# Projecting queries and keys of three head groups transposed, with one product moved to GpSimd and the values' matmuls ordered later

## The chip, the cores and the metric

The kernel runs on one core of a Trainium2 chip. The metric is device time in microseconds (us) of one execution. Engines are named as in the profile: PE is TensorE's matmul side and PEld its weight loads, DVE is VectorE, ACT is ScalarE, POOL is GpSimd, and SP issues nearly all DMAs. All engines take their instructions in program order, each from its own queue; the kernel is written in a tile framework that builds that order ahead of time from priorities and a timeline of its own, and inserts the semaphores.

## The reference

One residual block over 2048 rows of width 1024: RMSNorm, one projection, two kinds of attention side by side, an output projection, and a SwiGLU feed-forward part. Everything is float32. The change touches the stick-breaking half only:

```python
u = rms_norm(h, norm1_w[l])
proj = jnp.einsum('bsd,de->bse', u, w_in[l])
dq, dk, dv, sq, sk, sv = jnp.split(proj, SPLIT_POINTS, axis=-1)
...
z = jnp.einsum('bqhd,bkhd->bhqk', qb, k) * scale          # 8 heads of width 64
mask = (k_pos[None, :] < q_pos[:, None])[None, None]
log_1mb = jnp.where(mask, jax.nn.log_sigmoid(-z), 0.0)
rem = lax.cumsum(log_1mb, axis=3, reverse=True) - log_1mb
a = jnp.where(mask, jnp.exp(jax.nn.log_sigmoid(z) + rem), 0.0)
y = jnp.einsum('bhqk,bkhd->bqhd', a, v)
...
h = h + jnp.einsum('bse,ed->bsd', mix, w_out[l])
h = h + jnp.einsum('bsf,fd->bsd', jax.nn.silu(gate) * up, w_down[l])
```

In words: a weight a[t,s] is sigmoid(z[t,s]) times the product of (1 - sigmoid(z[t,j])) over the keys j between s and t. It is computed as a running product from the last key to the first.

## The kernel before

**Precision.** Matmuls run in float16 on split operands: a float32 value is a sum of a "hi" and a "lo" float16, and a product takes three of the four combinations (hi·hi, hi·lo, lo·hi). "Splitting" a tile means one cast (hi) and one subtraction (lo).

**Stages.** Eight head groups follow one another. Groups 0 to 3 are the four differential heads (`diff_attn`), groups 4 to 7 are two stick-breaking heads each (`sb_attn`). While group g is in attention, the rows of group g + 1 are projected in the gaps of PE: `advance` emits so many projection tiles (16 tiles of 128 rows each) for so much progress of the attention, and `PRI` gives the projection's matmuls a lower priority. Behind the attention of group 7 runs the output projection (`out_proj`), then the feed-forward part.

**Projection of a group** (`proj`, L379). For each tile of 128 rows `proj_tile` (L314) runs 24 matmuls: a 128x128 block of the rows, `xt`, is the stationary operand, and 384 columns of the weights stream (q, k and v of the group, 128 each). `proj_out` (L334) splits v into its tile and q, k into the tile `st`, straight out of PSUM. After every four tiles `proj_batch` (L348) turns q and k so that the head's dimensions lie on partitions: two DMA transposes (L372) write `qT[:, 2:4]` and `kT`, and two more DMAs (L374) copy `qT`'s two halves of partitions, exchanged, into `qT[:, 0:2]`. The hi parts of a head then lie on 64 partitions and the lo parts on the other 64, so that two matmuls make all four combinations. The PSUM pool `psj` has two banks, one for each tile's projection.

**Attention of a group** (`sb_attn`, L536). A unit is a block of 128 queries, i, one head, m, and a stretch, b, of up to 1024 keys: 48 units for a group. `stage_a` (L540) takes the stretch in chunks of 512 keys, the last chunk first. For each chunk `score_chunk` (L446) makes the scores with two matmuls into a PSUM bank `sc` (four banks); ACT makes 1 - beta into `om` (L554) and beta, in place in PSUM (L555); DVE makes the running product by a scan over `om` (L557) and then the product beta times the running product into `be` (L558). `split_t` (L398) splits the unit's `be`: ACT casts the hi part into the tile `s16` (three buffers), POOL subtracts for the lo part, and one DMA transpose (L403, on SP's queue) turns both into `aT` (six buffers), up to 16 blocks of 128x128. `stage_b` (L565) multiplies `aT` with v by `pv` (L453, matmuls of 64 columns at L458); it is emitted five units after its `stage_a` (`PD` = 5), and the framework is free to place it earlier or later among the scores. The tiles `be` and `om` come from one pool of nine, `z4`.

The pool `pp` has two buffers each of `st` (which groups 0 to 7 use in the projection) and `raw` (which groups 0 to 3 use there, and one step of the output weights at the end).

Of the kernel before, what the change touches and what calls it, by code (L numbers as in the profile page):

```python
# [59 lines left out]
def block(tc, a, out):  # L60
# [3 lines left out]
    with top:  # L64
# [44 lines left out]
        def nm(s):  # L109
            uid[0] += 1  # L110
            return f"{s}{uid[0]}"
# [14 lines left out]
        mhalf = c1(16, "mh")  # L126
        DVE.memset(mhalf[:], -0.5)

        def times(o, a_, b_, c=None):
# [121 lines left out]
        with ExitStack() as ph1:  # L251
# [62 lines left out]
            def proj_tile(G, xt):  # L314
# [7 lines left out]
                return pj  # L322

            def split_psum(hi, lo, src, n):
                sc = 2.0 ** -11
                if pick(A=0.84 * n + 60, D=1.05 * n + 70) == "A":
                    ACT.mul(hi, src, sc)
                else:
                    DVE.tensor_scalar(hi, src, sc, None, op0=ALU.mult)
                DVE.scalar_tensor_tensor(lo, src, sc, hi, op0=ALU.mult, op1=ALU.subtract)  # L330
                note("D", 1.05 * n + 70)

            @pri("po")
            def proj_out(g, G, pj, B, j):  # L334
# [9 lines left out]
                else:  # L344
                    split_psum(st[:, 0:4, j, 0, :], st[:, 0:4, j, 1, :], pj[:, :256].rearrange("p (c e) -> p c e", c=4), 256)

            @pri("pb")
            def proj_batch(g, G, B):  # L348
                st, v, raw = B
                qT = sp.tile([P, 4, 4, P], F16, tag="qT", bufs=QB, name=nm("qT"))  # L350
                kT = sp.tile([P, 2, 4, P], F16, tag="kT", bufs=KB, name=nm("kT"))
                if g < 4:
# [26 lines left out]
            def proj(g, G, fresh=None):  # L379
                for t in range(NT):  # L380
                    if fresh is not None:
                        feed(t)
                        xt = ahead.pop(0)
                    else:
                        xt = pp.tile([P, 2 * D], F16, tag="xt", bufs=3, name=nm("xt"))
                        SP.dma_start(xt[:], xs[t])
                    if t % 4 == 0:
                        st = pp.tile([P, 4, 4, 2, 64], F16, tag="st", name=nm("st"))
                        v = sp.tile([P, 4, 256], F16, tag="v", bufs=KB, name=nm("v"))
# [8 lines left out]
            def split_t(src, n, he="ADP", le="DP"):  # L398
# [4 lines left out]
                SP.dma_start_transpose(aT[:, : 2 * n // P, :], s16[:, : 2 * n])  # L403
                return aT
# [40 lines left out]
            @pri("sc")  # L445
            def score_chunk(G, sc, i, q, m, w, cut=False):  # L446
                for o in range(2):
                    PE.matmul(sc[:, : 128 * w].rearrange("p (t n) -> p t n", n=P), lhsT=G["q"][i // 4][:, 2 - 2 * o + m, i % 4, :], rhs=G["k"][q][:, m, 0:w, :], start=o == 0, stop=o == 1)  # L448
                if cut:
                    PE.matmul(sc[:, 128 * w - P : 128 * w], lhsT=idb[:], rhs=tri[:], start=False, stop=True, skip_group_check=True)  # L450

# [84 lines left out]
            def sb_attn(g, G):  # L536
                last = {}

                @pri("at")
                def stage_a(i, m, b):  # L540
# [8 lines left out]
                    for c in range((n - 1) // 512, -1, -1):  # L549
                        lo, hi = 512 * c, min(512 * c + 512, n)  # L550
                        w = hi - lo
                        sc = ps.tile([P, 512], F32, tag="sc", bufs=4, name=nm("sc"))
                        score_chunk(G, sc, i, 2 * b + c, m, w // P, b == i // 8 and hi == n)
                        ACT.activation(om[:, lo:hi], sc[:, :w], AF.Sigmoid, scale=G["nkz"][:])  # L554
                        ACT.activation(sc[:, :w], sc[:, :w], AF.Sigmoid, scale=G["kz"][:])  # L555
                        ov = om[:, lo:hi][:, ::-1]
                        DVE.tensor_tensor_scan(ov, ov, sc[:, :w], om[:, hi : hi + 1], op0=ALU.mult, op1=ALU.bypass)  # L557
                        DVE.tensor_tensor(be[:, lo:hi], sc[:, :w], om[:, lo + 1 : hi + 1], ALU.mult)  # L558
                        note("A", 1.7 * w + 400)
                        note("D", 3.15 * w + 350)  # L560
                    return n, split_t(be[:, :n], n, "A", "P")

                ypd = {}

                def stage_b(i, m, b, n, aT):  # L565
                    r, k = fq(g, i)
                    if i // k not in ypd:
# [660 lines left out]
```

## Time and profile before

| | |
|---|---|
| runs | 2734.09, 2731.22, 2727.44 us; median 2731.22 |
| profiled execution | 2740.3 us, its span 2738.5 us |
| mean granted TensorE clock | 0.967 |
| busy, share of the span | PE 91%, PEld 51%, DVE 72%, ACT 49%, POOL 52% |
| attention of groups 4, 5, 6, 7 begins at | 606, 794, 965, 1127 us |
| projections of groups 4, 5, 6, 7 begin at | 536, 686, 832, 987 us |
| last matmul of the values, first of the feed-forward part | 1396, 1458 us |

The attention's beginnings are those of each group's first scan (L557; there are 80 in a group), the projections' those of each group's first matmul at L320 (384 in a group). A line of the groups or of a window names first the program's line (L557), the engine and the operation, then the tiles, written and read, and the shapes; "x168" is the count; behind the bar stand the time in which any of them ran, the mean duration of one in ns, and the idle time of the engine right before them with what ended it. Matmuls are pipelined: a row's duration is longer than the distance to the next one, which is what a matmul costs in a run of them.

### The profile page before, as it was taken

To read this page: it belongs to the slowest core of one execution; us is meant where nothing else is said; L and a number is where in the kernel's file an instruction comes from. 1 tells how busy PE (TensorE), PEld (TensorE's weight loads), DVE (VectorE), ACT (ScalarE), POOL (GpSimd) and SP (SyncE) were. 2 spreads that over 40 slices of the span, in tenths; PEclk is the share of its full clock that TensorE was granted. 3 is DMA by queue.
4 is the path that set the end of the run, shared out by engine and by line. 5 is a ranking of instruction groups with operands and counts; after the bars stand their busy time and mean duration, and the time that the engine had idled before them with its cause. 6 is when DMAs were issued, how large, how long until landed. Compare 5 with 4: busy or idle time off the path is not lost.

```text
span 2738.5 us, 45414 instructions
## 1 busy us (share of the span) xinstructions
PE 2490.0 (91%) x17084; PEld 1409.8 (51%) x17084; DVE 1978.5 (72%) x3752; ACT 1353.3 (49%) x2539; POOL 1429.8 (52%) x1002
## 2 busy tenths in 40 slices
PE   7998989898978886889989898999999999999999
PEld 4655656565545553457775444444444444444444
DVE  6888879888888989987766777777786544434434
ACT  4665656566868778765644534344342212121121
POOL 2577677765554545546655566565664332222322
PEclk9999999998999997899999999999999999999999
DMA  6788787789998997997896665566657845635532
GB/s 227 199 164 178 151 198 164 180 171 200 208 201 184 212 186 151 203 192 208 213 289 256 220 234 191 208 221 216 231 204 283 316 158 181 220 128 193 192 116 93
DMA packets 646830, 543.52 MB, mean 198 GB/s; under 512 B 506369, under 2 KB 573953, under 8 KB 636369
## 3 DMA queue, kind: packets, MB, share of 16 engines
q1 hardware_dynamic: 644784, 538.53, 71.8%
q8 instruction: 134, 2.20, 0.3%
q0 software_dynamic: 512, 1.36, 0.2%
q10 hardware_dynamic: 1312, 0.72, 0.1%
q14 instruction: 88, 0.71, 0.1%
HBM read 261.08 MB, written 147.32 MB: 149 GB/s over the span
## 4 chain that ended last, share of the span: by engine, by line
PE 36%; DVE 9%; DMA 4%; POOL 3%; issue 3%; ACT 2%; SPq 0%; DVEq 0%; POOLq 0%; ACTq 0%
PE pd L1034 14%; PE pm L934 7%; PE pd L934 5%; PE pa L934 5%; DVE wd L215 2%; PE po L761 2%; DMA stages<-in_w_down_dram 1%; POOL stages L98 1%; DVE wu L215 1%; DMA aT<-s 1%; DVE z L557 1%; DVE cg L999 1%; DVE cg L98 1%; POOL s L98 1%; PE pj L320 1%
## 5 line engine op out<-in xcount | busy, mean ns | idle before, releaser
L98 POOL TENSOR_TENSOR s<-z,s 128x1024 f16<-128x1024 f32 (+7 forms) x288 | 474.4, 1655 | 320.1 <-ACT s L89 281.4
L320 PE MATMUL pj<-w,xt 128*128 128x384 f16 x3072 | 577.0, 336 | 19.2 <-DMA xt<-xs 5.6
L320 PEld LDWEIGHTS <-xt 128*128 128x128 f16 x3072 | 301.5, 101 | 233.1 <-issue 36.1
L557 DVE TENSOR_TENSOR_SCAN z<-z,sc 128x512 f32<-128x512 f32 (+3 forms) x320 | 356.1, 1114 | 72.1 <-ACT sc L555 68.8
L448 PE MATMUL sc<-kT,qT 128*128 128x512 f16 (+3 forms) x1280 | 348.3, 364 | 59.4 <-DVE z L558 23.7
L1034 PE MATMUL pd<-wd,act 128*128 128x512 f16 x1764 | 394.0, 381 | 7.2 <-DVE cu L968 7.1
L458 PE MATMUL yp<-v,aT 128*128 128x64 f16 (+1 forms) x4896 | 281.5, 209 | 82.3 <-DMA aT<-s 81.7
L458 PEld LDWEIGHTS <-aT 128*128 128x128 f16 x4896 | 245.4, 102 | 172.1 <-DMA aT<-s 110.4
L934 PEld LDWEIGHTS <-wg 128*128 128x128 f16 x1848 | 181.8, 98 | 228.1 <-issue 14.6
L934 PEld LDWEIGHTS <-wu 128*128 128x128 f16 x1848 | 180.8, 98 | 216.5 <-issue 2.0
L98 POOL TENSOR_TENSOR act<-cg,act 128x512 f16<-128x512 f32 x109 | 149.8, 1385 | 262.3 <-ACT act L993 262.3
L1034 PEld LDWEIGHTS <-act 128*128 128x128 f16 x1764 | 173.0, 98 | 216.6 <-issue 10.2
L89 ACT CAST s<-z 128x128 f16<-128x128 f32 (+7 forms) x216 | 170.3, 790 | 154.8 <-DMA aT<-s 72.9
L98 POOL TENSOR_TENSOR stages<-stages 128x512 f32<-128x512 f32 x97 | 172.9, 1783 | 120.1 <-DVE wg L215 41.4
L98 POOL TENSOR_TENSOR hs<-hs,cu 128x512 f32<-128x512 f32 x102 | 132.6, 1306 | 165.6 <-DVE hs L1040 62.7
L554 ACT ACTIVATE z<-sc,c 128x512 f32<-128x512 f32 (+3 forms) x320 | 204.4, 639 | 23.7 <-PE sc L448 18.9
L558 DVE TENSOR_TENSOR z<-sc,z 128x512 f32<-128x512 f32 (+3 forms) x320 | 193.7, 606 | 8.5
L555 ACT ACTIVATE sc<-sc,c 128x512 f32<-128x512 f32 (+3 forms) x320 | 196.5, 614 | 0.0
L1040 DVE SCALAR_TENSOR_TENSOR hs<-pd,c,hs 128x512 f32<-128x512 f32 x144 | 106.5, 748 | 118.5 <-PE pd L1034 113.6
L761 PE MATMUL po<-wo,mt 128*128 128x256 f16 x1536 | 180.7, 275 | 12.3 <-DVE xf L764 6.8
L993 ACT CAST act<-cg 128x512 f16<-128x512 f32 x126 | 76.9, 616 | 231.4 <-DVE cg L999 192.7
L934 PE MATMUL pm<-X,wu 128*128 128x512 f16 x792 | 179.1, 379 | 1.8 <-ACT cg L979 1.7
(241 smaller groups left out, 4109.1 us busy)
## 6 DMA issues: line engine op xcount, KB each, us to landing
xt<-xs SPq DMA_DIRECT2D x112, 512.0 KB, 4.4
hs<-hd SPq DMA_DIRECT2D x72, 512.0 KB, 4.5
hd<-hs SPq DMA_DIRECT2D x56, 512.0 KB, 5.8
split<-wg SPq DMA_DIRECT2D x11, 1792.0 KB, 6.9
split<-wu SPq DMA_DIRECT2D x11, 1792.0 KB, 6.7
split<-wd SPq DMA_DIRECT2D x11, 1792.0 KB, 6.8
wg<-split SPq DMA_DIRECT2D x11, 1792.0 KB, 7.4
wd<-split SPq DMA_DIRECT2D x11, 1792.0 KB, 9.1
```

Of the source, the lines that this page charges most:

```text
L89: ACT.copy(dst, src)
L98: (DVE if e == "D" else POOL).tensor_tensor(dst, a_, b_, op)
L320: PE.matmul(pj[:, :384], lhsT=xv[:, xi, kt, :], rhs=G["w"][:, wi, kt, :], start=n == 0, stop=n == 23)
L448: PE.matmul(sc[:, : 128 * w].rearrange("p (t n) -> p t n", n=P), lhsT=G["q"][i // 4][:, 2 - 2 * o + m, i % 4, :], rhs=G["k"][q][:, m, 0:w, ...
L458: PE.matmul(yp[:, y0 : y0 + wd], lhsT=aT[:, a_, :], rhs=v[:, v_ : v_ + wd], start=start and j == 0 and q == 0, stop=stop and j == nb - 1 a ...
L554: ACT.activation(om[:, lo:hi], sc[:, :w], AF.Sigmoid, scale=G["nkz"][:])
L555: ACT.activation(sc[:, :w], sc[:, :w], AF.Sigmoid, scale=G["kz"][:])
L557: DVE.tensor_tensor_scan(ov, ov, sc[:, :w], om[:, hi : hi + 1], op0=ALU.mult, op1=ALU.bypass)
L558: DVE.tensor_tensor(be[:, lo:hi], sc[:, :w], om[:, lo + 1 : hi + 1], ALU.mult)
L761: PE.matmul(po[:, sl], lhsT=mt[:, kt, P * xi : P * xi + P], rhs=wos[2 * h + n][wi][:, kt, :], start=q == 0, stop=q == 23)
L934: PE.matmul(ps_[:].rearrange("p (t n) -> p t n", n=P), lhsT=wv[:, wo, wi, 128 * kt : 128 * kt + 128], rhs=X[xo][:, :, xi, kt, :], start=st ...
L1034: PE.matmul(po[:], lhsT=act[:, ao, xi, 128 * j : 128 * j + 128], rhs=W["d"][:, wo, wi, :], start=start and u == 0 and q == 0, stop=u == nu ...
```

## The change

It has four parts, for groups 4 to 6 unless said otherwise.

1. `proj_turned` and `turned_out` take the place of `proj_tile`, `proj_out` and `proj_batch`. For q and k the weights are stationary and 128 rows stream, so q and k come out already turned; v is made as before. That is 72 matmuls of 128 columns for a tile instead of 24 of 384. q and k of two tiles share one PSUM bank, v of two tiles the other; both are emptied after the second tile. The splits write `qT` and `kT` directly; q is multiplied by a column, `half`, that is zero on the other head's partitions. The DMAs of `proj_batch` go, and `score_chunk` makes three matmuls for a chunk in place of two.
2. In chunks with c = 1 (the second 512 keys of a stretch) beta is written to `be` in SBUF, not in place in PSUM, and the product (L558) runs on POOL in place of DVE.
3. In groups 4 and 5 two of five units take `s16` from the tag `raw` and one of four takes `aT` from the tag `st`: five buffers in place of three, and eight in place of six.
4. In all four groups `stage_b`'s matmuls are put, on PE's queue, behind the last score matmul emitted so far. `stage_b` is emitted seven units after its `stage_a` in groups 4 and 5 (`lag` = `PD` + 2), five after in groups 6 and 7.

```diff
+        half = c1(2, "half")
+        DVE.memset(half[:], 0.0)
+        for m in range(2):
+            DVE.memset(half[64 * m : 64 * m + 64, m : m + 1], 2.0 ** -11)
...
+            def turned(g):
+                return 4 <= g < NG - 1
+
+            @pri("pm")
+            def proj_turned(G, xt, pq, pv, r):
+                xv = xt[:].rearrange("p (s k n) -> p s k n", s=2, k=KT)
+                for c in range(3):
+                    n = 0
+                    for kt in range(KT):
+                        for xi, wi in ((0, 0), (0, 1), (1, 0)):
+                            w_, x_ = G["w"][:, wi, kt, 128 * c : 128 * c + 128], xv[:, xi, kt, :]
+                            o = pv[:, P * r : P * r + P] if c == 2 else pq[:, 256 * c + P * r : 256 * c + P * r + P]
+                            PE.matmul(o, lhsT=x_ if c == 2 else w_, rhs=w_ if c == 2 else x_, start=n == 0, stop=n == 23)
+                            n += 1
+
+            @pri("po")
+            def turned_out(pq, pv, qT, kT, v, j):
+                two = slice(j - 1, j + 1)
+                q2, k2 = (pq[:, 256 * c : 256 * c + 256].rearrange("p (t n) -> p t n", t=2) for c in range(2))
+                for m in range(2):
+                    ACT.mul(qT[:, m, two, :], q2, half[:, m : m + 1])
+                    DVE.scalar_tensor_tensor(qT[:, 2 + m, two, :], q2, half[:, m : m + 1], qT[:, m, two, :], op0=ALU.mult, op1=ALU.subtract)
...
+                split_psum(kT[:, 0, two, :], kT[:, 1, two, :], k2, 256)
+                vv = v[:, two, :].rearrange("p t (h s e) -> p t h s e", h=2, s=2)
+                split_psum(vv[:, :, :, 0, :], vv[:, :, :, 1, :], pv[:, :256].rearrange("p (t h e) -> p t h e", t=2, h=2), 256)
...
+                        if t % 2 == 0:
+                            pq, pv_ = (psj.tile([P, 512], F32, tag="pj", name=nm("pj")) for _ in range(2))
+                        proj_turned(G, xt, pq, pv_, t % 2)
+                        if t % 2 == 1:
+                            turned_out(pq, pv_, qT, kT, v, t % 4)
...
-                s16 = s16p.tile([P, 2048], F16, tag="s16", bufs=SB, name=nm("s16"))
+                if wide is not None and wide % 5 in (1, 3):
+                    s16 = pp.tile([P, 4, 256], F32, tag="raw", name=nm("s16"))[:].rearrange("p t n -> p (t n)").bitcast(F16)
...
-                aT = sp.tile([P, 16, P], F16, tag="aT", bufs=AB, name=nm("aT"))
+                if wide is not None and wide % 4 == 3:
+                    aT = pp.tile([P, 4, 4, 2, 64], F16, tag="st", name=nm("aT"))[:].rearrange("p c t s e -> p (c t) (s e)")
...
-                for o in range(2):
-                    PE.matmul(sc[:, : 128 * w].rearrange("p (t n) -> p t n", n=P), lhsT=G["q"][i // 4][:, 2 - 2 * o + m, i % 4, :], rhs=G["k"][q][:, m, 0:w, :], start=o == 0, stop=o == 1)
+                terms = ((m, 0), (2 + m, 0), (m, 1)) if turned else ((2 + m, m), (m, m))
+                for o, (a_, b_) in enumerate(terms):
+                    last = PE.matmul(sc[:, : 128 * w].rearrange("p (t n) -> p t n", n=P), lhsT=G["q"][i // 4][:, a_, i % 4, :], rhs=G["k"][q][:, b_, 0:w, :], start=o == 0, stop=o == len(terms) - 1)
...
+                lag = PD + 2 if g < NG - 2 else PD
...
+                        front.append(score_chunk(G, sc, i, 2 * b + c, m, w // P, b == i // 8 and hi == n, turned(g)))
+                        aside = c == 1 and turned(g)
+                        beta = be[:, lo:hi] if aside else sc[:, :w]
-                        ACT.activation(sc[:, :w], sc[:, :w], AF.Sigmoid, scale=G["kz"][:])
+                        ACT.activation(beta, sc[:, :w], AF.Sigmoid, scale=G["kz"][:])
...
-                        DVE.tensor_tensor(be[:, lo:hi], sc[:, :w], om[:, lo + 1 : hi + 1], ALU.mult)
+                        (POOL if aside else DVE).tensor_tensor(be[:, lo:hi], beta, om[:, lo + 1 : hi + 1], ALU.mult)
...
+                    return n, split_t(be[:, :n], n, "A", "P", wide[0] if g < NG - 2 else None)
...
                 def stage_b(i, m, b, n, aT):
+                    with tc.issue_after(front[-1]):
+                        stage_c(i, m, b, n, aT)
...
-                            if len(pend) > PD:
+                            if len(pend) > lag:
```

`stage_c` is the body that `stage_b` had. The numbers by which the framework's balance of work between engines is reckoned (`note`) change with the work.

More of the change, by code (lines that the diff above doesn't have):

```diff
@@ L345, in proj_out, with new_qk @@
                     split_psum(st[:, 0:4, j, 0, :], st[:, 0:4, j, 1, :], pj[:, :256].rearrange("p (c e) -> p c e", c=4), 256)
+            def new_qk():
+                qT = sp.tile([P, 4, 4, P], F16, tag="qT", bufs=QB, name=nm("qT"))
+                kT = sp.tile([P, 2, 4, P], F16, tag="kT", bufs=KB, name=nm("kT"))
+                return qT, kT
             @pri("pb")
@@ L349, in proj_batch @@
                 st, v, raw = B
[L350 to L351 removed]
+                qT, kT = new_qk()
                 if g < 4:
@@ L445, in score_chunk @@
             @pri("sc")
-            def score_chunk(G, sc, i, q, m, w, cut=False):
-                for o in range(2):
-                    PE.matmul(sc[:, : 128 * w].rearrange("p (t n) -> p t n", n=P), lhsT=G["q"][i // 4][:, 2 - 2 * o + m, i % 4, :], rhs=G["k"][q][:, m, 0:w, :], start=o == 0, stop=o == 1)
+            def score_chunk(G, sc, i, q, m, w, cut=False, turned=False):
+                terms = ((m, 0), (2 + m, 0), (m, 1)) if turned else ((2 + m, m), (m, m))
+                for o, (a_, b_) in enumerate(terms):
+                    last = PE.matmul(sc[:, : 128 * w].rearrange("p (t n) -> p t n", n=P), lhsT=G["q"][i // 4][:, a_, i % 4, :], rhs=G["k"][q][:, b_, 0:w, :], start=o == 0, stop=o == len(terms) - 1)
                 if cut:
-                    PE.matmul(sc[:, 128 * w - P : 128 * w], lhsT=idb[:], rhs=tri[:], start=False, stop=True, skip_group_check=True)
+                    last = PE.matmul(sc[:, 128 * w - P : 128 * w], lhsT=idb[:], rhs=tri[:], start=False, stop=True, skip_group_check=True)
+                return last.ins
             @pri("pv")
```

28 lines of the change are left out of this document (23 added, 5 removed).

## The prediction

> **What bounds the kernel now.** I read the page first: PE is busy for 91% of the span. That is no answer for the stages that change, so I cut the run into windows at the first scan of each group. Each row gives the stretch, its length, the busy time (and count) of PE, PEld, DVE, ACT and POOL, the granted clock, the DMA engines' share and GB/s.
>
> ```profile
> 536.00:606.00 70.00, 66.50 (x541) 43.03 (x542) 65.89 (x196) 43.67 (x114) 46.92 (x33) 0.98 0.78 159
> 606.00:794.00 188.00, 161.97 (x1598) 102.53 (x1596) 166.12 (x309) 146.22 (x287) 102.03 (x63) 0.94 1.02 207
> 794.00:965.00 171.00, 140.20 (x1420) 86.83 (x1418) 151.78 (x268) 133.61 (x252) 86.20 (x54) 0.91 0.99 195
> 965.00:1127.00 162.00, 123.71 (x1299) 76.04 (x1296) 149.52 (x251) 131.17 (x246) 83.86 (x55) 0.85 0.87 173
> ```
>
> These are the end of group 3's attention and the attentions of groups 4, 5 and 6. In groups 4 and 5 the DMA engines are at 1.02 and 0.99 (packets overlap, so the share can pass 1); in group 6 they are at 0.87, and DVE is at 149.52 of 162 us. Then the waits of 606 to 1127 us (who, on what: total, times, longest) and that stretch's DMAs:
>
> ```profile
> POOL s L98 <- ACT s L89: 217.1, 101, 7.2
> PEld L458 <- DMA aT<-s: 61.5, 54, 3.4
> PE yp L458 <- DMA aT<-s: 44.8, 42, 2.9
> ACT s L89 <- DMA aT<-s: 44.0, 34, 3.9
> DVE z L557 <- ACT sc L555: 38.0, 42, 4.6
> PE sc L448 <- DVE z L558: 18.3, 21, 2.4
> ```
>
> ```profile
> DMA packets 266988, 100.18 MB, mean 192 GB/s; under 512 B 244321, under 2 KB 258740, under 8 KB 266932
> q1 hardware_dynamic: 266932, 99.44, 95.6%
> qT<-qT SPq DMA_DIRECT2D x24, 128.0 KB, 2.7
> aT<-s SPq DMA_TRANSPOSE x146, 4.4
> qT<-st SPq DMA_TRANSPOSE x12, 3.4
> kT<-st SPq DMA_TRANSPOSE x12, 3.7
> ```
>
> The transpose of the weights, `aT`, is late for two readers: PE, which has the values' matmuls in its queue ahead of the next scores, and ACT, whose cast wants an `s16` buffer back. While ACT stands, the sigmoids behind the cast stand, and DVE's scan waits for those (38.0 us). So groups 4 and 5 are held by the transposes' round trip, group 6 by DVE.
>
> **The change part by part.**
>
> *DMAs that go.* A batch of four tiles has two transposes of 128x1024 float16 (0.524 MB) and two copies of 128 KB (0.262 MB). By bytes, 99.44 MB cost 0.956 x 521 = 498 us, so 0.786 MB cost 3.9 us; by packets, 2048 transposed rows of 256 bytes and 128 of 2 KB at 498 / 266932 us cost 4.1 us. I take 4.0. How many batches lie in each stage follows from the projection's matmuls in it, 96 to a batch:
>
> ```profile
> 606.00:794.00 188.00, 100.05 (x521) 51.71 (x522) 0.94 1.02 207
> 794.00:965.00 171.00, 75.83 (x407) 39.87 (x404) 0.91 0.99 195
> 965.00:1127.00 162.00, 44.34 (x240) 22.81 (x240) 0.85 0.87 173
> ```
>
> That is 5.4, 4.2 and 2.5 batches, the last partly group 7's, which keep their DMAs: 22, 17 and about 4 us of DMA time go. 1.02 x 188 = 192 becomes 170, 169 becomes 152, 141 becomes 137. Their issue goes from SP's queue too, where `aT`'s transposes stand behind it.
>
> The Trainium skill's page "DMA: Bandwidth & Descriptors", section "Latency and other measured facts", gives a DMA transpose 261 GB/s; 0.524 MB would then cost 2.0 us against 2.7 at the 192 GB/s of the row above, and the relief in groups 4 and 5 would be some 7 us less in all. The row is of this kernel, mixed with its other packets, so I stay with it.
>
> *DVE and POOL.*
>
> ```profile
> L557 DVE TENSOR_TENSOR_SCAN z<-z,sc 128x512 f32<-128x512 f32 x224 | 285.3, 1274 | 37.1 <-ACT sc L555 35.3
> L558 DVE TENSOR_TENSOR z<-sc,z 128x512 f32<-128x512 f32 x224 | 153.6, 686 | 5.2
> L98 POOL TENSOR_TENSOR hs<-hs,cu 128x512 f32<-128x512 f32 x102 | 132.6, 1306 | 165.6 <-DVE hs L1040 62.7 <-DVE cu L1040 45.4 <-issue 44.8
> L98 POOL TENSOR_TENSOR s<-z,s 128x1024 f16<-128x1024 f32 x120 | 262.6, 2193 | 153.9 <-ACT s L89 146.3 <-issue 4.0 <-POOL s L98 1.2
> L330 DVE SCALAR_TENSOR_TENSOR v<-pj,v 128x128 f16<-128x128 f32 x128 | 35.2, 278 | 10.6 <-ACT v L327 10.4
> L330 DVE SCALAR_TENSOR_TENSOR st<-pj,st 128x256 f16<-128x256 f32 x64 | 26.0, 408 | 2.9 <-ACT st L327 2.9
> L327 ACT ACTIVATE st<-pj 128x256 f16<-128x256 f32 x64 | 24.9, 393 | 13.7 <-DVE v L330 13.4 <-PE sc L450 0.3
> ```
>
> Chunks with c = 1 hold, for one head, 1280 columns in blocks 4 to 7, 2048 in 8 to 11, 2048 + 1280 in 12 to 15: 6656, for two heads 13312, or 26 chunks of 512 (32 instructions). DVE loses 26 x 0.686 = 17.8 us a group. POOL gains 26 x 1.306 = 34 us: 102, 86 and 84 become 136, 120 and 118. POOL stands idle for 217 us behind the casts, so there is room; ahead of the product nothing but POOL's own subtraction can stand, behind it that unit's cast waits. Emptying two projected tiles takes DVE 4 x 408 in place of 2 x (278 + 408): +0.26 us, 2 us a group; ACT the same. Net, DVE goes from 166, 152, 150 to 150, 136, 134; ACT from 146, 134, 131 to 148, 136, 133. Writing beta to SBUF and not PSUM I bound by the two sigmoids' rows, 705 to SBUF and 681 ns to PSUM at 512 columns: under 1 us a group, taken as nothing.
>
> *PE.* The next rows are start, length and count; a matmul costs the distance to the next piece's start.
>
> ```profile
> 579.32 1.95 PE L458 MATMUL yp<-v,aT 128*128 128x128 f16 x32
> 581.10 1.14 PE L320 MATMUL pj<-w,xt 128*128 128x384 f16 x6
> ...
> 822.01 0.60 PE L448 MATMUL sc<-kT,qT 128*128 128x512 f16 x2
> 822.44 0.98 PE L458 MATMUL yp<-v,aT 128*128 128x64 f16 x28
> 823.26 1.95 PE L320 MATMUL pj<-w,xt 128*128 128x384 f16 x11
> ...
> 825.43 2.28 PE L320 MATMUL pj<-w,xt 128*128 128x384 f16 x13
> 827.54 0.25 PE L458 MATMUL yp<-v,aT 128*128 128x64 f16 x3
> ```
>
> 128 columns with a new stationary block each cost 1.78 / 32 = 56 ns, 384 cost 2.11 / 13 = 162, a score of 512 costs 215, a values' matmul 29. A projected tile goes from 24 x 162 = 3.89 us to 72 x 56 = 4.03: +2 us a group. The third score pass is 34816 columns a group, 68 x 0.215 = 14.6 us. In all 17 us a group, 50 in the three. PE's columns now (projection + 136 x 0.215 + some 820 x 0.029) are 137, 119 and 92 us; they become 154, 136 and about 108. With 188, 171 and 162 us to lie in, the addition hides behind DMA, DVE and ACT; if that cover goes, it costs up to 50.
>
> *Emptying PSUM.* Both `psj` banks serve one pair of tiles, so the next pair waits for six reads (three on ACT, three on DVE, some 0.4 us each, among scans of 1.3). Nothing shows this wait; nothing to 2 us for each of 24 pairs. PE can run scores and values meanwhile, except under group 3's attention, where PE is busy for 66.5 of 70 us: I take +2 us there. `load_w` takes its `psj` bank after tile 8, so in the middle of a pair, and now waits for that pair to be emptied; its weights are wanted eight tiles later, some 80 us, so I cost that at nothing.
>
> *More buffers, later values.*
>
> ```profile
> L403 SPq DMA_TRANSPOSE aT<-s x288: 1167/1782/6046, 113.9 to 1388.4; - x144
> DMA to landing us min/median/max: 2.3/4.3/9.0
> ```
>
> A transpose lands in 4.3 us (9.0 at most). Seven units at the stages' 188 / 48 = 3.9 and 3.6 us are 25 us from scores to values, so the 45 us of PE's waits and the 44 of ACT's should mostly go in groups 4 and 5. What is late next is ACT: a full unit has two chunks of 705 + 681 ns and a cast of 1053, about 3.8 us.
>
> ```profile
> L554 ACT ACTIVATE z<-sc,c 128x512 f32<-128x512 f32 x224 | 157.9, 705 | 16.8 <-PE sc L448 14.9 <-PE sc L450 1.4 <-POOL s L98 0.4
> L555 ACT ACTIVATE sc<-sc,c 128x512 f32<-128x512 f32 x224 | 152.5, 681 | 0.0
> L89 ACT CAST s<-z 128x1024 f16<-128x1024 f32 x83 | 87.4, 1053 | 71.3 <-DVE z L558 19.7 <-DMA aT<-s 15.2 <-issue 13.7
> ```
>
> The new order makes PE hold ready values back while scores wait for a bank of `sc`; those waits are 18.3 us now and should get shorter with the shorter DVE. `finish` moves with the values: its transposes on PE, and behind them its few DVE, ACT and POOL instructions and one DMA of 256 KB on SP for four blocks of queries come up to two units later, past the next units' transposes on SP; nobody reads `ms` before group 7, so nothing there. In group 7 the last values come up to two units later (each 24 x 0.029 = 0.7 us): +1.5.
>
> *Sum.* Group 4: next bounds are DMA 170, PE 154, DVE 150; 188 becomes 172 (-16). Group 5: DMA 152, DVE 136, PE 136; 171 becomes 157 (-14). Group 6: DMA 137, DVE 134, ACT 133; today's 12 us above its busiest engine grow to about 18, as it has no more buffers and a third score pass: 162 becomes 155 (-7). With +2 and +1.5 that is -33.5. The profiled execution took 2740.3 us, 9 above the median of the runs shown, 2731.2; so 2707 for a profiled run, 2698 for the median.
>
> **The rivals.**
>
> 1. *The third pass is bare.* For it: PE waits for DVE before scores (18.3 us) and its order is now fixed. Against it: PE's columns fill at most 154 of 172 us. Half of 50 us on the path: -33.5 + 25, 2722.
> 2. *The transposes never bound.* The page "Perfetto Trace Analysis" of the Trainium skill, section "Identifying the Most-Contended Engine", calls the DMA engines' occupancy misleading; by it my 1.02 proves nothing. As a mechanism: the latency of a transpose, not the engines' load, made the waits, and the buffers and DVE alone help. Then groups 4 and 5 give some 5 us each: -17 + 3.5, 2717. Against it: landing takes 4.3 us at the median, 2.3 at least.
> 3. *POOL's queue, the slower one.* The new product may stand behind a subtraction that waits for ACT's cast; that cast waits for a product. POOL waits 217.1 / 101 = 2.15 us a time there. If of each of the 96 new products more than 33.5 / 96 = 0.35 us stays on the path, the gain is gone; a quarter of 2.15 gives 96 x 0.54 = 52, so 2731 - 33.5 + 52 = 2750. For it: the 7.2 us at the longest. Against it: product and last chunk run apart, and nine `z4` tiles hold four units.
> 4. *Weight loads bind.* 72 loads a tile at 98 ns, one after the other, would be 7.1 us against 3.9: 150 us in 48 tiles, half of it bare: over 2770. The run of 32 above, at 56 ns with a load each, speaks against it.
> 5. *Nothing comes of it*: ACT, at 148 of 172, holds each stage where it is: 2731.
>
> **How the numbers follow.** The forecast has 0.58 (alone 2675 to 2718: all of 50 us relieved, or 13). Rival 1 has 0.15, rival 2 0.08, rival 3 0.13, rival 4 0.03, rival 5 0.03. About 0.2%, 5.5 us, can be told from no change. Faster: 0.58 + 0.10 of rival 1 + 0.07 of rival 2 = 0.75; slower: 0.13 + 0.03 + 0.02 of rival 1 + 0.02 of rival 5 = 0.20; the rest, 0.05, the same. The range reaches from a little under the forecast's own, 2668, to rival 3's 2752, and leaves out about 0.1 above and 0.03 below.
>
> **What would show it.** Right: in the attentions of groups 4 and 5 the DMA share under 0.95, PE's and ACT's waits on `aT` together under 30 us, DVE about 16 us less in each stage, L458 waiting for nothing. Wrong: POOL's product waiting on POOL's subtraction with ACT's cast behind it (rival 3); PE above 95% busy with long runs at the score line (rival 1); the projection's matmuls of 128 columns more than 60 ns apart (rival 4); pairs of tiles waiting for `psj`.

## The result and the profile after

The changed kernel takes 2706.61 us at the median (2704.82 to 2710.16, four runs); the kernel before took 2732.65 (2727.44 to 2736.76, four runs). The ratio is 0.9907 with a 95% interval of 0.9894 to 0.992: 26 us, just under 1%, faster. The forecast was 2698, 33.5 us faster than the 2731.2 that it started from. The profiled execution of the changed kernel has a span of 2702.7 us.

The page after, and the attentions of groups 4, 5 and 6 cut at their first scans (stretch, length, PE, PEld, DVE, ACT, POOL, clock, DMA share, GB/s):

```profile
span 2702.7 us, 50511 instructions
PE 2500.8 (93%) x19628; PEld 1502.5 (56%) x19628; DVE 1956.5 (72%) x3711; ACT 1346.4 (50%) x2488; POOL 1516.4 (56%) x1097
```

```profile
602.00:762.00 160.00, 145.90 (x2227) 118.37 (x2224) 148.18 (x256) 138.93 (x259) 123.26 (x92) 0.98 0.94 185
762.00:920.00 158.00, 141.26 (x2237) 113.89 (x2235) 143.99 (x250) 132.73 (x242) 116.21 (x88) 1.00 0.95 185
920.00:1092.00 172.00, 153.31 (x2096) 115.62 (x2092) 151.26 (x267) 131.37 (x238) 117.96 (x89) 0.97 0.92 187
```

Group 4 went from 188 to 160 us, group 5 from 171 to 158, group 6 from 162 to 171. The DMA engines fell from 1.02 and 0.99 to 0.94 and 0.95 although the stages are shorter; PE's clock rose from 0.94, 0.91 and 0.85 to 0.98, 1.00 and 0.97. The main waits of 602 to 1092 us (line numbers are now those of the changed kernel: L341 is the turned projection, L363 the lo parts out of its banks, L506 the scores, L517 the values, L619 the second sigmoid, L621 the scan, L622 the product):

```profile
POOL z L622 <- DVE z L621: 64.0, 49, 4.0
POOL s L98 <- ACT s L89: 49.1, 40, 4.9
ACT s L89 <- DMA aT<-s: 18.9, 12, 3.6
PEld L517 <- DMA aT<-s: 13.6, 15, 2.4
PE sc L506 <- DVE z L622: 12.1, 17, 1.6
PE yp L517 <- DMA aT<-s: 10.4, 12, 2.3
```

PE's wait on `aT` fell from 44.8 to 10.4 us, ACT's from 44.0 to 18.9. POOL's wait for ACT's cast fell from 217.1 to 49.1 us; it now waits mainly for the scan (L621) that feeds its new product (L622).

### The profile page after: what moved, and what is told of

Its sections match the earlier page's. It is cut to its first block, busy times and chain, and to the rows that moved or that the text cites. A ratio compares the mean times of both kernels' runs of the same rounds, so it can differ in the third digit from the quotient of the medians.

```text
span 2702.7 us, 50511 instructions
## 1 busy us (share of the span) xinstructions
PE 2500.8 (93%) x19628; PEld 1502.5 (56%) x19628; DVE 1956.5 (72%) x3711; ACT 1346.4 (50%) x2488; POOL 1516.4 (56%) x1097
## 5 line engine op out<-in xcount | busy, mean ns | idle before, releaser
L506 PE MATMUL sc<-kT,qT 128*128 128x512 f16 (+3 forms) x1520 | 381.6, 353 | 53.5 <-DVE z L622 19.0
L621 DVE TENSOR_TENSOR_SCAN z<-z,sc 128x512 f32<-128x512 f32 (+3 forms) x320 | 352.8, 1112 | 56.7 <-ACT sc L619 34.9
L325 PE MATMUL pj<-w,xt 128*128 128x384 f16 x1920 | 353.1, 332 | 17.2 <-ACT raw L374 5.9
L1004 PEld LDWEIGHTS <-wg 128*128 128x128 f16 x1848 | 181.5, 98 | 226.1 <-issue 12.4
L1004 PEld LDWEIGHTS <-wu 128*128 128x128 f16 x1848 | 181.5, 98 | 220.2 <-issue 7.1
L517 PE MATMUL yp<-v,aT 128*128 128x64 f16 (+1 forms) x4896 | 269.1, 204 | 37.3 <-DMA aT<-s 36.2
L517 PEld LDWEIGHTS <-aT 128*128 128x128 f16 x4896 | 236.9, 99 | 115.4 <-DMA aT<-s 47.7
L325 PEld LDWEIGHTS <-xt 128*128 128x128 f16 x1920 | 187.5, 99 | 146.9 <-issue 23.3
L98 POOL TENSOR_TENSOR stages<-stages 128x512 f32<-128x512 f32 x97 | 171.6, 1769 | 119.1 <-DVE wg L220 41.3
L618 ACT ACTIVATE z<-sc,c 128x512 f32<-128x512 f32 (+3 forms) x320 | 210.6, 663 | 25.1 <-PE sc L506 12.5
L506 PEld LDWEIGHTS <-qT 128*128 128x128 f16 x1520 | 128.2, 99 | 121.4 <-issue 23.5
L341 PE MATMUL pj<-xt,w 128*128 128x128 f16 x2304 | 176.9, 222 | 6.2 <-DVE v L363 5.2
```

What stands on the lines that cost most here:

```text
L98: (DVE if e == "D" else POOL).tensor_tensor(dst, a_, b_, op)
L325: PE.matmul(pj[:, :384], lhsT=xv[:, xi, kt, :], rhs=G["w"][:, wi, kt, :], start=n == 0, stop=n == 23)
L341: PE.matmul(o, lhsT=x_ if c == 2 else w_, rhs=w_ if c == 2 else x_, start=n == 0, stop=n == 23)
L506: last = PE.matmul(sc[:, : 128 * w].rearrange("p (t n) -> p t n", n=P), lhsT=G["q"][i // 4][:, a_, i % 4, :], rhs=G["k"][q][:, b_, 0:w, :] ...
L517: PE.matmul(yp[:, y0 : y0 + wd], lhsT=aT[:, a_, :], rhs=v[:, v_ : v_ + wd], start=start and j == 0 and q == 0, stop=stop and j == nb - 1 a ...
L1004: PE.matmul(ps_[:].rearrange("p (t n) -> p t n", n=P), lhsT=wv[:, wo, wi, 128 * kt : 128 * kt + 128], rhs=X[xo][:, :, xi, kt, :], start=st ...
```

## The experiments

All ratios are to the kernel before, on the same chip, with their 95% intervals. The table gathers the stages from one profiled execution of each kernel, from first scan to first scan, in us; group 7 ends at its last scan. "Turned" is the turned projection with its three score passes, "product" the product on POOL, "order" the values behind the scores, "buffers" the extra `s16` and `aT` with the seven units.

| kernel | ratio | group 4 | 5 | 6 | sum | group 7 |
|---|---|---|---|---|---|---|
| before | 1 | 187.5 | 171.6 | 162.0 | 521 | 255 |
| turned alone | 1.0009 | 179.5 | 168.5 | 176.7 | 525 | 250 |
| product alone | 1.0006 | 185.4 | 165.4 | 154.5 | 505 | 265 |
| product, order | 0.9925 | 186.6 | 161.5 | 151.2 | 499 | 250 |
| product, order, five `s16` | 0.9979 | 183.4 | 167.4 | 158.0 | 509 | 264 |
| turned, product, order | 0.9956 | 166.1 | 162.0 | 178.3 | 506 | 257 |
| turned, product, buffers | 0.9954 | 169.1 | 166.3 | 177.2 | 513 | 261 |
| turned, buffers | 1.0033 | 181.5 | 169.2 | 181.8 | 532 | 259 |
| turned, order, buffers | 1.0149 | 177.6 | 183.6 | 193.2 | 554 | 263 |
| all (the changed kernel) | 0.9907 | 160.2 | 158.2 | 171.4 | 490 | 258 |

One caution stands over the table. Group 7 has almost the same work in all of them, and its stage takes 250 to 265 us. The framework places the whole program anew after each edit, and I take these 15 us for what placing alone can move in a total; no run shows that by itself. I therefore read the parts from the stages they touch, and a difference of 15 us between two totals is not yet evidence for a mechanism.

**1. Without the product on POOL.**

```diff
-                        aside = c == 1 and turned(g)
+                        aside = False
```

> The changed kernel with the c = 1 products back on DVE; everything else of the change stays. Theory (DVE's relief is needed, ACT and DVE are the next bounds): DVE's busy time in the attentions of groups 4, 5, 6 goes back up by 18 us each, from 148, 144, 151 to about 166, 162, 169, and the stages, now 160, 158 and 171 us, can't be shorter than that: some 25 us of the 26 gained are lost, ratio to before 0.998 to 1.003. Rival 3 (the product on POOL costs waits): the kernel gets faster without it, ratio 0.988 or less. Rival 2 (DVE was not what counted): ratio stays at 0.990 to 0.993.

Measured: ratio 1.0149 (1.0129 to 1.0169), 41 us slower than the kernel before. The product is worth some 67 us inside the changed kernel, more than the DVE work it takes away, and the theory was 25. (The edit also puts beta of these chunks back into its PSUM bank, which stays in use until DVE's product is done; no run separates this from the work that DVE takes back.) DVE is near its limit, at 92%, in group 4 alone:

```profile
609.00:786.00 177.00, 152.81 (x2287) 123.72 (x2285) 162.07 (x277) 142.74 (x267) 98.88 (x62) 0.96 0.84 174
786.00:970.00 184.00, 144.50 (x2072) 115.00 (x2070) 155.13 (x265) 136.04 (x251) 85.40 (x54) 0.92 0.76 151
970.00:1163.00 193.00, 163.91 (x2233) 123.89 (x2234) 163.59 (x286) 141.62 (x268) 88.80 (x57) 0.96 0.79 172
```

In groups 5 and 6 DVE is at 84 and 85%, the DMA engines at 0.76 and 0.79: something else holds these stages. Experiment 12 came from this.

**2. Without the extra buffers and the seven units; 3. without the order; 4. without the turned projection (and the buffers).**

```diff
-                lag = PD + 2 if g < NG - 2 else PD
+                lag = PD                                  # 2 and 4, with split_t's wide = None
...
-                    with tc.issue_after(front[-1]):       # 3
-                        stage_c(i, m, b, n, aT)
+                    stage_c(i, m, b, n, aT)
...
-                return 4 <= g < NG - 1                    # 4, the product on POOL kept
+                return False
```

> The changed kernel without the two tags' extra buffers and with the values five units behind in all groups; the order on PE stays. Theory (the transposes' round trip is what the buffers hide, in groups 4 and 5): the waits of PE and ACT on aT, 17 us in these two groups now, come back in part, to 30 to 50 us, and 8 to 15 us are lost: ratio 0.9935 to 0.996. If the order on PE alone, with five units, is enough (group 6 has no more than that and its waits on aT are 13 us): ratio 0.990 to 0.992, no loss.

> The changed kernel without the order on PE's queue: the values are emitted seven and five units after their scores, but the framework may place their matmuls earlier. Theory (the framework believes the transposes earlier than they land and puts values ahead of scores that could run): in groups 4 and 5, where the delay falls back to some five units, PE's waits on aT rise from 5 us to 15 to 30, and 5 to 10 us are lost: ratio 0.9925 to 0.9945. Rival (the order only ties PE's hands): the same or faster, 0.9905 or less.

> The kernel before with the c = 1 products on POOL and the order on PE, values five units behind; the projection, the DMAs of q and k and the two score passes are as before, so it differs from the kernel without the extra buffers by the turned projection alone. Theory (the DMA engines bind groups 4 and 5): slower than that kernel by 12 to 25 us, DMA share back at 1.0 in group 4; ratio 0.999 to 1.003. Rival 1 (the third score pass is bare): faster than that kernel by up to 15 us, ratio 0.986 to 0.990. Rival 2 (the DMA engines' load never bound): within 5 us of it.

Measured: 0.9956 (0.9944 to 0.9969), 0.9954 (0.9938 to 0.9969) and 0.9925 (0.9912 to 0.9938). Without the buffers 13 us go, within the expected range; without the order 13 us go, more than the expected 5 to 10. Where the order is missing, PE stands before late transposes again, in the waits of 600 to 1113 us of that kernel:

```profile
PEld L517 <- DMA aT<-s: 63.2, 45, 5.5
PE yp L517 <- DMA aT<-s: 52.0, 40, 5.0
ACT s L89 <- DMA aT<-s: 23.2, 16, 3.4
```

The fourth kernel is a miss for the theory: it is faster than the second, from which it differs by the turned projection alone, by about 0.3%. It bears out none of the three expectations whole. Group 4 does get longer with the old projection, 166 to 187 us, as the DMA theory has it, with the DMA share back at 0.97. But group 5 stays at 162, at the same share, and group 6 gets shorter, 178 to 151. The first rows are the stages with the old projection; the next count the projection's matmuls in each stage of the changed kernel, whose group 7 projects at L325 as before:

```profile
604.00:791.00 187.00, 159.23 (x1577) 102.78 (x1574) 158.52 (x305) 138.42 (x255) 128.97 (x95) 0.95 0.97 206
791.00:952.00 161.00, 134.36 (x1419) 85.30 (x1419) 142.36 (x261) 128.42 (x232) 111.75 (x86) 0.96 0.97 204
952.00:1103.00 151.00, 119.90 (x1268) 73.87 (x1268) 135.28 (x235) 126.66 (x229) 111.86 (x86) 0.86 0.86 184
```

```profile
602.00:762.00 160.00, 71.00 (x1110) 64.35 (x1110) 0.98 0.94 185
762.00:920.00 158.00, 71.21 (x1124) 64.14 (x1121) 1.00 0.95 185
920.00:1092.00 172.00, 54.46 (x793) 49.28 (x793) 0.97 0.92 187
...
920.00:1092.00 172.00, 28.93 (x168) 15.92 (x168) 0.97 0.92 187
```

At 72 (turned) and 24 matmuls a tile the changed kernel projects 15, 16 and 18 tiles in the three stages; the kernel before, and the one with the old projection, project 22, 17 and 10. The old projection runs far ahead under group 4 and leaves ten tiles for group 6; the turned one spreads evenly. So the turned projection moves eight tiles, some 32 us of PE, out of groups 4 and 5 into group 6, and one stage alone misprices it.

The fourth kernel says more: the product and the order alone, with the old projection and all its DMAs in place, give 20 of the 26 us. What the turned projection and the buffers add to it together is 5 us, by ratios whose intervals overlap.

**5. The DMAs put back as load.**

```diff
+                if j == 3 and g >= 5:
+                    bh = bias[:].rearrange("p h n -> p (h n)").bitcast(F16).rearrange("p (s c n) -> p s c n", s=2, n=P)
+                    d2 = sp.tile([P, 7, P], F16, tag="d2", bufs=1, name=nm("d2"))
+                    for q in range(2):
+                        SP.dma_start_transpose(bh[:, q], v[:].rearrange("p t n -> p (t n)"))
+                    for o in (0, 64):
+                        SP.dma_start(d2[o : o + 64].rearrange("p c n -> p (c n)"), bh[64 - o : 128 - o, 0, 0:7].rearrange("p c n -> p (c n)"))
```

> The changed kernel, and for each batch of four tiles of groups 5 and 6 (8 of the 12 batches) two DMA transposes of 128x1024 float16 and two copies (112 KB each) are issued on SP as before the change, from v into space that nobody reads: their load without anybody's wait. 8 x 4.0 us = 32 us of DMA time come back between 602 and 1092 us. Theory (the DMA engines' load binds groups 4 and 5, now at 0.94 and 0.95): DMA share at 1.0 or over, some 12 to 20 us lost, ratio 0.995 to 0.998. Rival 2 (only the latency of a transpose counted, and the buffers hide it): 4 us at most, ratio 0.9905 to 0.992.

Measured: 0.9962 (0.9948 to 0.9976), 15 us lost. The total is within the theory's range; the stages do not bear the theory out. The rows are the three stages, then the put-back transposes issued in each of them (two to a batch), then what SP's queue waited for at the transposes (L360) and the copies (L362) that were put back (L628 is the scan in this kernel):

```profile
601.00:760.00 159.00, 145.15 (x2234) 117.91 (x2232) 145.90 (x252) 138.94 (x259) 123.99 (x93) 0.99 0.94 189
760.00:920.00 160.00, 141.27 (x2235) 114.24 (x2233) 143.86 (x248) 132.71 (x240) 116.34 (x88) 0.99 1.05 197
920.00:1102.00 182.00, 157.35 (x2102) 118.22 (x2099) 152.56 (x277) 133.36 (x240) 118.92 (x89) 0.96 0.92 199
```

```profile
bias<-v SPq DMA_TRANSPOSE x2, 3.9
bias<-v SPq DMA_TRANSPOSE x8, 4.3
bias<-v SPq DMA_TRANSPOSE x6, 4.3
```

```profile
SPq L360 <- DVE z L628: 7.0, 5, 3.1
SPq L362 <- DMA bias<-v: 4.1, 3, 1.9
SPq L360 <- DVE z L614: 3.4, 2, 2.3
SPq L360 <- DVE y L493: 2.2, 1, 2.2
```

By shares and lengths the DMA engines work 485 us here against 459 in the changed kernel, 26 us for eight batches of 0.75 MB: 3.3 us each, where the prediction took 4.0 for 0.79 MB. Four batches fall into group 5's stage. They bring 18 us of DMA time and a share of 1.05, and the stage grows by 2.5 us, from 158.2 to 160.7. Group 4's stage, with one batch, gets 2 us shorter. Of the 11 us lost in the three stages 10.5 lie in group 6, where the share is 0.92 as in the changed kernel. So a share above 1 did not hold group 5, and what the 15 us are stays open. Nor is it load alone that was put back: SP's queue, in which `aT`'s transposes stand behind the new DMAs, waited 17 us at them. Rival 2 and the placing both remain.

**6. Two score passes in place of three.**

```diff
-                terms = ((m, 0), (2 + m, 0), (m, 1)) if turned else ((2 + m, m), (m, m))
+                terms = ((m, 0), (2 + m, 0)) if turned else ((2 + m, m), (m, m))
```

> The changed kernel with two score passes in groups 4 to 6: the product of q's hi part with k's lo part is left out. 44 us of PE go. If the third pass hides behind DMA, DVE and ACT, as forecast: 5 us at most, ratio 0.9885 to 0.9907. Rival 1 (it is bare, for half or more): 15 to 35 us faster, ratio 0.978 to 0.985; that the kernel with the old projection was 8 us faster than its turned pair points this way.

Measured: 0.9892 (0.9872 to 0.9911), some 4 us faster than the changed kernel, whose 0.9907 lies inside this interval; the sum of the three stages is 489 against 490. The 44 us of the third pass are hidden but for about that much, and rival 1, which had 15 to 35 us, falls. The pass does move work: without it 19, 17 and 14.5 tiles are projected in the three stages (15, 16 and 18 with it), group 6 falls from 171 to 166 us and group 4 grows from 160 to 167.

**7. The product on POOL alone; 8. the turned projection alone.** Number 7 is the kernel before with the product's lines of the diff; number 8 is the changed kernel with the edits of 1, 2 and 3 together.

> The kernel before with the c = 1 products of groups 4 to 6 on POOL and nothing else. DVE loses 18 us a group. If the DMA engines bind groups 4 and 5, these barely move and group 6 gains some 10: ratio 0.995 to 0.997. If DVE's work was what counted in all three groups, as the 67 us that the product was worth in the changed kernel suggest: 20 us or more, ratio 0.990 to 0.9927, and the order on PE, which is what this lacks against the kernel with 0.9925, is worth little without the turned projection.

> The kernel before with the turned projection (and the three score passes) in groups 4 to 6 and nothing else: products on DVE, no order on PE, three and six buffers, values five units behind. Theory as formed by now: the turned projection by itself costs time, since its pair of tiles keeps both PSUM banks until DVE and ACT have emptied them, and a busy DVE empties late; then the projection is barely ahead of the attention and the attention waits for it. Slower than before by 20 to 45 us, ratio 1.007 to 1.017, with the last projected tile less than 15 us ahead of the block that needs it, where it was 40 to 120 us ahead before. The forecast's step (22 + 17 + 4 us of DMA time go, 17 us of PE a group hide): faster, ratio 0.990 to 0.996.

Measured: 1.0006 (0.9993 to 1.0018) and 1.0009 (0.9993 to 1.0024). Neither does anything to the total by itself, and none of the expected ratios came. With the turned projection alone the lead over the attention did fall, to 10 us at the least in group 6, and cost nothing in the total. The two profiles suggest why (first the product alone, then the turned projection alone):

```profile
605.00:790.00 185.00, 157.12 (x1539) 99.34 (x1538) 157.79 (x302) 137.82 (x255) 126.92 (x93) 0.96 1.00 205
790.00:955.00 165.00, 133.99 (x1458) 84.26 (x1455) 141.59 (x260) 130.30 (x230) 114.62 (x87) 0.98 1.03 206
955.00:1110.00 155.00, 122.51 (x1268) 76.93 (x1268) 136.20 (x237) 127.07 (x230) 112.66 (x86) 0.85 0.92 178
```

```profile
601.00:781.00 180.00, 154.30 (x2331) 125.39 (x2329) 165.33 (x283) 144.34 (x271) 95.66 (x62) 0.96 0.85 174
781.00:949.00 168.00, 144.31 (x2232) 116.17 (x2230) 155.33 (x264) 135.63 (x250) 87.18 (x54) 0.98 0.84 170
949.00:1126.00 177.00, 152.27 (x2039) 111.31 (x2037) 161.03 (x283) 138.75 (x264) 88.66 (x57) 0.97 0.85 182
```

With the product moved, the DMA engines stand at 1.00 and 1.03 and groups 4 and 5 take 185 and 165 us. With the DMAs gone, the share is 0.85, but DVE is at 91 to 92% of each stage and groups 4 and 5 take 180 and 168. I read this as two limits side by side, either of which alone holds the stage. The table agrees in group 4: 188 us before, 183 to 187 in the kernels with the product and the old projection, 178 to 182 in the turned ones without the product, 160 to 169 with both. In groups 5 and 6 it shows no such pattern, and group 6 is longer in every turned kernel than in the kernel before.

That the one limit is the DMA engines' load is not shown. With the turned projection six tiles, some 24 us of PE, leave group 4 as well. And the share is not a fixed load: the product alone and the product with the order move the same 99 MB in the three stages, and by shares and lengths this took 498 us in the one and 467 in the other.

The product alone did shorten the three stages by 16 us; group 7, which it does not touch, took 10 us more.

**9. Five `s16` buffers without the turned projection.** The kernel of number 4, with `raw` as in the change for groups 4 to 6.

> The kernel before with the c = 1 products on POOL, the order on PE, values five units behind, and five buffers of s16 in groups 4 to 6 (from the tag raw): the parts of the change that need no turned projection. ACT waited 44 us for an s16 there with three buffers; if a third to a half of that was on the path, 8 to 15 us are gained on 0.9925: ratio 0.987 to 0.9895, faster than the changed kernel. If the DMA engines bind (0.97 in groups 4 and 5), buffers move nothing: 0.992 to 0.9925.

Measured: 0.9979 (0.997 to 0.9989), slower than the same kernel with three buffers, 0.9925. The expected 8 to 15 us did not come; by the table 9 us were lost in the three stages and 14 in group 7. The buffers add no instruction, so I suspect the placing. What exactly went wrong I have not settled.

**10. More room in PSUM for the pairs; 11. emptying first.** The changed kernel projects barely ahead of the attention: from the last matmul of a tile's projection to the first score of that block of queries there pass 9 us at the least in group 6, where it was 96 us before. I took this for a new limit, and the two banks of the pairs for its cause. In the edits, the first pair of lines is number 10, the second number 11.

```diff
-                            pq, pv_ = (psj.tile([P, 512], F32, tag="pj", name=nm("pj")) for _ in range(2))
+                            pq, pv_ = psj.tile([P, 512], F32, tag="pj", name=nm("pj")), ps.tile([P, 512], F32, tag="pvb", bufs=1, name=nm("pvb"))   # and "sc" has bufs=3
...
-PRI = {"sc": 0, "spl": 0, "pv": 0, "fin": 0, "pm": -200, "po": 0, "pb": 0, "lw": 0, "fr": 0, "at": 200, "ox": 0, "wm": 0}
+PRI = {"sc": 0, "spl": 0, "pv": 0, "fin": 0, "pm": -200, "po": 400, "pb": 0, "lw": 0, "fr": 0, "at": 200, "ox": 0, "wm": 0}
```

> The changed kernel with q and k of the pairs alone in the two psj banks, v in a bank of its own that is taken from the scores (three sc banks in place of four, in all groups). If the banks hold the projection back, it gets ahead of the attention again (over 20 us at the least, where it is 9 us in group 6 now), and group 6's stage falls from 171 us to some 160: ratio 0.985 to 0.989, less what a bank fewer costs the scores. If PE itself, full at 150 of 160 us, holds it back: no gain, and the missing sc bank costs 5 to 15 us, ratio 0.9925 to 0.997.

> The changed kernel with the emptying of the projection's banks put ahead of other work in the framework's order (the priority po from 0 to 400; in all groups). The time from a pair's last matmul to its q and k emptied, 4.8 us at the median now and 12.5 at the most, falls; if the banks hold the projection back, group 6's stage falls by 5 to 10 us, ratio 0.987 to 0.9895. If PE holds it back: within 4 us of the changed kernel, 0.990 to 0.992.

Measured: 1.0045 (1.003 to 1.0059) and 0.9989 (0.9975 to 1.0003). With its own banks the projection does get ahead, to 71 us at the least in group 6, and its work goes back under groups 4 and 5 (the turned projection's matmuls in each stage):

```profile
611.00:784.00 173.00, 86.13 (x1335) 77.13 (x1333) 0.98 0.92 186
784.00:949.00 165.00, 81.95 (x1250) 73.02 (x1248) 0.98 0.95 180
949.00:1122.00 173.00, 22.81 (x347) 19.87 (x344) 0.95 0.82 179
```

Group 6 still takes 173 us, with only five turned tiles left in it beside eight of group 7's. Not having the projection ahead is not what holds the changed kernel; this theory falls, as far as a run can say that also took a bank from the scores. In the eleventh, emptying took no less time (5.3 us at the median, 4.8 before the edit), and 15 of its 22 us were lost before group 4's first scan, in groups that the change does not touch but whose emptying the new priority covers too.

**12. Without the product and without the order.** The edits of 1 and 3 together.

> The changed kernel with the c = 1 products back on DVE and without the order on PE's queue: turned projection, more buffers, values emitted seven and five units after their scores. It asks why the changed kernel without the POOL product lost 1.5% against the kernel before, when the turned projection alone lost nothing. If the order on PE does it (with DVE slow, PE holds ready values back while scores wait for DVE): the loss goes, ratio 0.996 to 1.003, and group 6's stage falls from 193 us to some 177. If the buffers and the seven units do it: ratio 1.010 or more.

Measured: 1.0033 (1.0016 to 1.005). Without the product on POOL, taking the order away gains 32 us, where with the product it loses 13. Its stages come to 532 against 554 us. The ratio is just above the range expected if the order does it, and group 6 is at 182 rather than 177. Waits that differ, in the kernel with the order (786 to 1163 us) and in the one without (781 to 1131 us); "issue" is idle time in which the engine waited for nothing that the profile shows:

```profile
DVE z L621 <- ACT sc L619: 37.3, 24, 6.5
PEld L341 <- issue: 25.5, 10, 6.3
PE pj L341 <- DVE v L363: 22.7, 6, 6.2
PE yp L517 <- DMA aT<-s: 4.4, 4, 2.4
```

```profile
PE yp L517 <- DMA aT<-s: 15.7, 17, 3.5
DVE z L621 <- ACT sc L619: 13.7, 16, 3.2
PEld L341 <- issue: 8.6, 10, 3.9
PE pj L341 <- DVE v L363: 1.6, 3, 0.7
```

The order saves 11 us of waits on `aT` and costs 21 us of waits of the projection for a bank that DVE has not emptied, up to 6.2 us at a time; I take it that the next scores, and so the scan, stand behind them. The weights' step of `load_w`, which takes the same banks, waits 12 us for one with the order and 5 without. Where DVE is relieved the emptying comes in time: in the changed kernel the projection waits 5 us for its banks in all three stages. This is how the rows read; that the banks' waits alone make the 32 us was not tried.

## Why the prediction was right

**The whole.** -33.5 us was forecast and -26 measured, in the forecast's own range. In the profiled pair the three stages went from 521 to 490, -31 against -37 forecast. The total was right; of the mechanism a part was borne out, a part was not, and some luck was in it, as follows. The product and the order, without the part that was to relieve the DMA engines, give 20 of the 26 us (4).

**DMAs.** 22 + 17 + 4 = 43 us of DMA time were to go. By shares and lengths the three stages had 502 us and now have 459: 43. The match is closer than such sums can bear, as the same bytes took 498 and 467 us in two kernels (7). That this load bound groups 4 and 5 is not shown: put back, it cost 15 us, but not in the stage in which most of it landed (5). Rival 2's mechanism stays open, though not its 5 us a group. The Trainium skill, "Perfetto Trace Analysis", section "Identifying the Most-Contended Engine", calls the occupancy of the DMA engines misleading; here the trace agrees: group 5 went to a share of 1.05 and grew by 2.5 us.

**DVE and POOL.** The direction was right, the size was not. The sum of DVE was to fall from 468 to 420; it fell from 467 to 443. The product itself went as reckoned: 96 of them took 91 us on POOL, 30 us a group against 34. But the step "DVE loses 17.8 us a group, and emptying costs 2" left out the program's own balance: `split_psum` picks the engine of each hi part by reckoned load, and with DVE relieved on paper it chose DVE. That line's 17 us on DVE are most of the 23 that are missing. These rows are the line on ACT before (606 to 1127 us; it had none on DVE), then on DVE and on ACT after (602 to 1092 us):

```profile
606.00:1127.00 521.00, 33.16 (x98) 0.90 0.96 192
```

```profile
602.00:1092.00 490.00, 16.97 (x43) 0.98 0.94 186
...
602.00:1092.00 490.00, 4.24 (x9) 0.98 0.94 186
```

**PE.** A matmul of 128 columns with its own weights takes 56 ns in the turned projection too:

```profile
710.70 2.96 PE L341 MATMUL pj<-xt,w 128*128 128x128 f16 x50
713.49 0.67 PE L341 MATMUL pj<-w,xt 128*128 128x128 f16 x9
```

The next piece starts 2.79 us later, and 2.79 us for 50 is 56 ns; rival 4 falls. The cover of the third pass was real (6).

**Buffers and order.** Under 30 us of waits on `aT` were forecast for PE and ACT together in groups 4 and 5, and 17 came. The two parts are worth 13 us each, in the company of the other parts. Of the other signs, the DMA share came to 0.94 and 0.95, the second not quite under 0.95; DVE lost 18 us in group 4 but 8 in group 5, where 16 was forecast; and the values' matmuls still waited 5 us for `aT` in the two groups.

**The stages, where the sum was mis-sized.** Group 4 gave -27 for -16, group 5 -13 for -14, group 6 +9 for -7. The step that failed is "PE's columns", which left the 5.4, 4.2 and 2.5 batches where they were: the projection no longer runs ahead, and eight tiles moved into group 6. The third pass is a part of it, since without it 3.5 of the eight left group 6 again (6), and the pairs' banks are another, since with a bank of its own for v five did (10). That these tiles make group 6's +9 is not shown: in number 10 the stage stayed at 173 us without the five, though with one score bank fewer. In the sum the two errors met, 11 us too much gained in group 4 and 16 too little in group 6; that is luck.

**The small terms.** In the changed kernel's three stages PE waits 5 us for the pairs' banks, where nothing to 2 us a pair was allowed, and 6 us for `load_w`'s, which was put at nothing. Group 3's end was to lose 2 us and gained 4; group 7's end lost 3 where 1.5 was said, within what placing alone moves.

**Rival 3.** POOL's product hardly held up the unit: in groups 4 and 5 ACT's cast waited 3.5 us for it and 4.1 for POOL's subtraction. Without the product the other three parts together lose 41 us (1).

## What to carry to other kernels

Where two resources of a stage stand within a few per cent of each other, an edit that relieves one can come to nothing, and that is no verdict on the edit: try the two together before dropping either, and also without the rest, since two of the four parts gave most of the gain here. When a load is put back that nobody waits for, see in which stage it lands and in which one the time is lost, and whether the queue that issues it is held up as well; the total alone does not tell throughput from latency. And price a change in the sum of the stages that share its work, since work without a due date moves to wherever the other engines leave room.

## What was not expected

The same order on PE's queue gained 13 us in one company and lost 32 in another. The product of two SBUF tiles took POOL 1135 ns for 512 columns, where the sum of two float32 tiles elsewhere in this kernel takes 1306; what makes the difference is not shown. And an ACT cast out of PSUM with a column as its scale took 519 ns for 256 columns, against 396 with a constant in the kernel before; that the column makes the difference was not tried.

```profile
L622 POOL TENSOR_TENSOR z<-z,z 128x512 f32<-128x512 f32 x60 | 68.1, 1135 | 46.3 <-DVE z L621 35.5 <-DVE z L607 6.0 <-DVE c L176 1.7
L349 ACT ACTIVATE qT<-pj,half 128x256 f16<-128x256 f32 x42 | 21.8, 519 | 11.6 <-PE pj L341 8.4 <-DVE qT L350 3.2
```
